# Reordered tokens and half-width keys in the first attention of a two-layer decoder kernel

## The chip, the cores and the metric

The kernel runs on one core of one Trainium2 chip. The time is the device time of one execution in microseconds (us), as the median of several runs. A profile is one execution taken by the hardware profiler.

## The reference

One sequence of 256 tokens, width 2048, two layers in float32. What matters here is the attention of the first layer, a mixture of three dilated windows with 8 heads of width 128 each:

```python
DILATED_GROUPS = ((128, 1), (512, 4), (2048, 16))     # window, distance
qkv = (xn @ w_in).reshape(B, S, 3, G * Hg, dh)        # G = 3 groups, Hg = 8 heads
q, k, v = rope(q) * dh ** -0.5, rope(k), v
for g, (window, dil) in enumerate(DILATED_GROUPS):
    idx = t[:, None] - dil * jnp.arange(window // dil + 1)[None, :]     # keys t, t - dil, ...
    s = where(idx >= 0, q[g] . k[g][idx], NEG_INF)
    lse = logsumexp(s); out = exp(s - lse) @ v[g][idx]
o = sum over g of softmax(lse over g) * out           # one softmax over all three groups' keys
h = h + o.reshape(S, Hg * dh) @ w_out
```

Then the first layer's MLP (2048 to 8192 and back) and gate, the shared keys and values, the second attention, its MLP and gate, and a last norm. With 256 tokens the second group sees the earlier keys whose distance is a multiple of 4, the third those at a multiple of 16, the first all keys up to 128 back.

## The kernel before

All large products are split: a float32 weight is cast to fp32r ("whi", ScalarE, line 198) and the rest is kept as "wlo" (VectorE, line 204), and activations are split likewise into two halves of one tile ("xa"). A weight comes in blocks of 128 x 1024 (512 KB), issued on SP's queue in program order (`load`, line 186). `Program.run` goes through a list of steps, keeps the loads some blocks ahead and the casts and splits three to four blocks ahead of the matmuls, and lets generators of other work advance by one `yield` between blocks. The schedule is written by hand: the instructions of each engine run in the order in which the program issues them. `prog.until` advances the generators until a condition holds.

x lies feature-major in SBUF, as eight tiles `xp[j]` of 128 features x (2 x 256 tokens). It is loaded once (`load_x`, line 180), squared and split at the start, and the out-projection later adds to it in place.

The first attention: `v_unit(0)` first, then for each head six `single` units (queries and keys of three groups, 16 blocks of 128 rows, lines 327 and 329), with the previous head's `a_scores` behind unit 1, `a_transpose` behind unit 3 and `a_pv` behind unit 4. Value units of 512 columns (`token_major`, lines 418 to 420) stand between heads: unit 1 after head 0, 2 after head 1, 3 after head 3, 4 after head 4, 5 in head 7. Value columns are ordered head by head, three groups each, so that a unit holds four (head, group) pairs. The rows of v for tokens 0 to 127 are kept split ("v0", two parts), those for 128 to 255 plain ("v1").

Tokens are in natural order. With two halves of 128 tokens, queries of the first half see only keys of the first, queries of the second see both. For each group the scores are a plain f32 product of 128 x 128 for the first half (line 717) and one of 128 x 256 for the second (line 718), 1152 columns of probabilities in all. They are masked (line 727), exponentiated (732), scaled (736), transposed on TensorE (746 to 749), copied out and split where both halves of the queries need them (754 to 757). `a_pv` makes, for each group, three split products with 256 columns (line 771: hi x hi, hi x lo, lo x hi) with the values of tokens 0 to 127 and one plain f32 product with 128 columns (769, 774) for queries and keys of the second half. `split_to` (448, 450) writes the head's output as hi and lo to "oT".

PSUM is two rings: "mm", four banks one at a time (`bank`), and "at", two pairs of banks (`banks2`). Scores and transposes take a pair and a bank each. The out-projection takes all four "mm" banks for its first 512 columns, and the last two heads' `a_pv` run behind its first and second weight block.

Of the kernel before, what the change touches and what calls it, by code (L numbers as in the profile page):

```python
# [10 lines left out]
F32 = mybir.dt.float32  # L11
F32R = mybir.dt.float32r
# [28 lines left out]

def f32(ap):
    return ap.bitcast(F32)


class Program:
# [87 lines left out]
def kernel(ctx: ExitStack, tc: tile.TileContext, a: dict, out: bass.AP):  # L134
# [40 lines left out]
    warm = const.tile([P, 1], F32, name="warm")  # L175
    nc.scalar.copy(warm, ones[:, :1])

    def load_x(j, half=None):
        c = slice(0, 2 * T) if half is None else slice(half * T, (half + 1) * T)
        nc.sync.dma_start(xp[j][:, c], a["xT"][:, j * 2 * T:(j + 1) * 2 * T][:, c])  # L180


    def load(n, src):
# [263 lines left out]
    def split_to(dst, src):  # L447
        nc.scalar.copy(dst[:, :T], src)
        yield
        nc.vector.tensor_sub(dst[:, T:], src, f32(dst[:, :T]))  # L450
# [194 lines left out]
    def start0():  # L645
        load_x(0, 0)
        load_x(0, 1)
        ps = bank()
        for _ in range(WARM_UP):
            nc.tensor.matmul(ps[:, :P], ones, ones, start=True, stop=True)  # L650
        open_pool("A")
        pa = cur["A"]
        cur["mA0"] = pa.tile([P, NGA * P], F32, name="mA0")
        cur["mA1"] = pa.tile([P, NGA * T], F32, name="mA1")

    def tables():
        nc.sync.dma_start(ident, a["ident"])
        nc.sync.dma_start(ropeC, a["ropeC"])
        nc.sync.dma_start(ropeS, a["ropeS"])
        nc.sync.dma_start(cur["mA0"], a["mA0"])  # L660
        nc.sync.dma_start(cur["mA1"], a["mA1"])
    prog.op(start0)

    def start_x(k):
# [4 lines left out]
    def square_pair(j):  # L669

        pa = cur["A"]
        if j == 0:
            cur["sum2"] = pa.tile([P, NGA * (P + T)], F32, name="p", tag="p")[:, :2 * T]
# [23 lines left out]
    def v_done(u, j, ps):  # L697
        while n_a0.r is None:
            yield
        v = cur["A"].tile([P, 512], F32, tag="v1", name="v1", bufs=3) if j else \  # L700
            cur["A"].tile([P, 2, 512], F32R, tag="v0", name="v0", bufs=3)
        col = n_a0.col[:, j:j + 1]
        nc.scalar.activation(v if j else v[:, 0], ps, AF.Identity, scale=col)
        if not j:
            yield
            nc.vector.scalar_tensor_tensor(v[:, 1], ps, col, f32(v[:, 0]), op0=ALU.mult, op1=ALU.subtract)
        va[u, j] = v

    sm = {}

    def a_scores(h):
        prog.until(lambda: ready.get(h) == 6)
        sb = banks2()
        flat, s0 = sb.rearrange("p a b -> p (a b)"), bank()
        for g in range(NGA):
            q, k = qk[h][:, g * T:(g + 1) * T], qk[h][:, (3 + g) * T:(4 + g) * T]
            nc.tensor.matmul(s0[:, g * P:(g + 1) * P], q[:, :P], k[:, :P], start=True, stop=True)
            nc.tensor.matmul(flat[:, g * T:(g + 1) * T], q[:, P:], k, start=True, stop=True)  # L718
        yield
        pa = cur["A"]  # L720
        p = pa.tile([P, NGA * (P + T)], F32, tag="p", name="p")
        s4 = pa.tile([P, 4], F32, tag="s4", name="s4", bufs=2)
        lo, parts = 0, []
        for j, (src, mask) in enumerate(((s0, cur["mA0"]), (flat, cur["mA1"]))):
            w = mask.shape[1]
            parts.append(p[:, lo:lo + w])
            nc.vector.tensor_tensor_reduce(out=parts[j], in0=src[:, :w], in1=mask, scale=-SCALE, scalar=3e38,
                                           op0=ALU.add, op1=ALU.min, accum_out=s4[:, j:j + 1])
            lo += w
        yield  # L730
        for j, d in enumerate(parts):
            nc.scalar.activation(d, d, AF.Exp, bias=s4[:, j:j + 1], scale=-1.0, accum_out=s4[:, 2 + j:3 + j])
        yield
        nc.vector.reciprocal(s4[:, 2:4], s4[:, 2:4])
        for j, d in enumerate(parts):
            nc.vector.tensor_scalar_mul(d, d, s4[:, 2 + j:3 + j])
        sm[h] = p

    def a_transpose(h):
        prog.until(lambda: h in sm)  # L740
        p = sm.pop(h)
        sb = banks2()
        flat, t0 = sb.rearrange("p a b -> p (a b)"), bank()
        w = NGA * P
        for g in range(NGA):
            nc.tensor.transpose(flat[:, g * T:g * T + P], p[:, g * P:(g + 1) * P], ident)
            nc.tensor.transpose(flat[:, g * T + P:(g + 1) * T], p[:, w + g * T:w + g * T + P], ident)
        for g in range(NGA):
            nc.tensor.transpose(t0[:, g * P:(g + 1) * P], p[:, w + g * T + P:w + (g + 1) * T], ident)
        yield  # L750
        pt = cur["A"].tile([P, NGA, 2, T], F32R, tag="pt", name="pt", bufs=2)
        pl = cur["A"].tile([P, w], F32, tag="pl", name="pl", bufs=2)
        early = flat[:, :NGA * T].rearrange("p (g t) -> p g t", g=NGA)
        nc.scalar.copy(pt[:, :, 0, :], early)
        nc.scalar.copy(pl, t0[:, :w])
        yield
        nc.vector.tensor_sub(pt[:, :, 1, :], early, f32(pt[:, :, 0, :]))
        sm[h, "T"] = pt, pl

    def a_pv(h, wide=False):  # L760
        units = {divmod(3 * h + g, 4)[0] for g in range(NGA)}
        prog.until(lambda: (h, "T") in sm and all((u, j) in va for u in units for j in range(2)))
        pt, pl = sm.pop((h, "T"))
        pv = (banks2()[:, 0, :] if wide else bank())[:, :T]
        for g in range(NGA):
            u, c = divmod(3 * h + g, 4)
            c = slice(c * P, (c + 1) * P)
            if g:
                nc.tensor.matmul(pv[:, P:], va[u, 1][:, c], pl[:, g * P:(g + 1) * P], start=False, stop=False)
            for vp, pp in ((0, 0), (0, 1), (1, 0)):  # L770
                nc.tensor.matmul(pv, va[u, 0][:, vp, c], pt[:, g, pp, :], start=g == vp == pp == 0,
                                 stop=g == NGA - 1 and vp == 1)
            if g == 0:
                nc.tensor.matmul(pv[:, P:], va[u, 1][:, c], pl[:, :P], start=False, stop=False)
# [12 lines left out]
    for h in range(HA):  # L787
        for i in range(6):
# [466 lines left out]
    return v.T.reshape(k // P, P, -1).transpose(1, 0, 2).reshape(P, -1)  # L1255


def _tables():
    f = np.float32
    inv = f(500000.0) ** (-np.arange(16, dtype=f) * f(2.0 / 32))  # L1260
# [6 lines left out]

    c, s = cs(t)
    tab = {"ropeC": c.T, "ropeS": s.T, "ident": np.eye(P, dtype=f)}
    cmp_pos = np.minimum(np.arange(16), 14) * 16 + 31  # L1270
# [5 lines left out]
    tab["mA0"] = np.concatenate([m[:P, :P] for m in add], 1)  # L1276
    tab["mA1"] = np.concatenate([m[P:, :] for m in add], 1)
# [9 lines left out]
def _layout(i):  # L1287
    a = dict(_tables())
    a["xT"] = _feature_major(i["x"][0])
    a["pT"] = np.stack([_feature_major(i["p"][l, 0]) for l in range(2)])  # L1290
# [5 lines left out]
    a["w_v"] = _quads(w[:, 2].transpose(0, 2, 1, 3).reshape(D, -1))  # L1296
# [37 lines left out]
```

## Time and profile before

| | |
|---|---|
| median of 3 runs | 2513.28 us (2513.19 to 2513.33) |
| profiled execution | 2514.11 us |
| its span | 2511.3 us |
| TensorE granted clock, mean | 0.999 |
| TensorE (PE) busy | 2500.4 us, 13497 matmul records |
| VectorE (DVE) busy | 1662.3 us |
| ScalarE (ACT) busy | 1351.0 us |
| DMA | 466.10 MB, mean 186 GB/s |

How to read the rows: PE is TensorE's matmuls, PEld its weight loads, which overlap the matmuls; SPq is the sequencer that issues transfers. "mm<-qk" means that tile mm is written from tile qk, L717 is line 717 of the kernel before. A plain f32 matmul appears as two records, an fp32r one and a transpose as one. Matmuls are pipelined, so a record's duration reaches into the next one. A timeline row has start, duration, engine, line, operation, tiles and shape, and "xN" merges N records. A row of the waits has the total in us, the number of times, and the longest. A row of a source line has the shortest, median and longest duration in ns, then the first and last start. A row of windows has the stretch, its length, the busy us (with the number of instructions) of PE, PEld, DVE, ACT and POOL, the granted clock, the DMA engines' share and GB/s.

### The profile page before, as it was taken

How to read it: one execution, taken by the hardware profiler on the slowest of the kernel's cores; microseconds unless marked ns; L12 is line 12 of the kernel's file. 1: busy time of each engine (PE TensorE's matmuls, PEld its weight loads, DVE VectorE, ACT ScalarE, POOL GpSimd, SP SyncE). 2: the span in 40 equal slices, each digit the busy share in tenths (PEclk: the TensorE clock that was granted, in tenths of full speed). 3: DMA queues.
4: the chain of work that ended last, by engine and by line, in shares of the span. 5: the costliest groups of instructions: out<-in, count | busy, mean ns of one | idle time of the engine just before them, and what ended most of it. 6: DMA issues, size and time to landing. Idle time of an engine off the chain costs nothing.

```text
span 2511.3 us, 36082 instructions
## 1 busy us (share of the span) xinstructions
PE 2500.4 (100%) x13497; PEld 2156.5 (86%) x13497; DVE 1662.3 (66%) x2808; ACT 1351.0 (54%) x2168; POOL 10.4 (0%) x24
## 2 busy tenths in 40 slices
PE   9999999999999999999999999999999999999998
PEld 8888888888888888888888889888888888888887
DVE  7766677865465565566787989766546556556676
ACT  6444444554454453455564788755545445445455
POOL 0000000000000000000000000000000000000000
PEclk9999999999999999999999999999999999999999
DMA  7555545556555655555565753455555655665553
GB/s 272 172 179 178 175 161 181 173 188 193 193 188 193 191 192 193 192 192 185 186 195 189 243 163 121 141 191 190 192 192 188 193 192 192 193 192 190 182 189 121
DMA packets 130111, 466.10 MB, mean 186 GB/s; under 512 B 14608, under 2 KB 15888, under 8 KB 129936
## 3 DMA queue, kind: packets, MB, share of 16 engines
q1 hardware_dynamic: 129264, 462.68, 56.6%
q8 instruction: 105, 1.72, 0.3%
q0 software_dynamic: 528, 1.07, 0.2%
q14 instruction: 70, 0.57, 0.1%
q10 hardware_dynamic: 144, 0.07, 0.0%
HBM read 461.65 MB, written 2.10 MB: 185 GB/s over the span
## 4 chain that ended last, share of the span: by engine, by line
PE 99%; DVE 0%; DMA 0%; SPq 0%; ACT 0%; issue 0%; DVEq 0%
PE mm L327 22%; PE at L327 17%; PE mm L329 11%; PE at L329 9%; PE mm L418 6%; PE mm L420 6%; PE mm L419 6%; PE at L420 5%; PE at L418 5%; PE at L419 5%; PE at L1180 0%; PE at L718 0%; PE mm L1204 0%; PE mm L938 0%; PE mm L939 0%; DMA raw<-in_w_v 0%
## 5 line engine op out<-in xcount | busy, mean ns | idle before, releaser
L204 DVE TENSOR_TENSOR wlo<-raw,whi 128x1024 fp32r<-128x1024 f32 (+1 forms) x875 | 1065.7, 1219 | 634.3 <-PE at L420 131.5
L198 ACT CAST whi<-raw 128x1024 fp32r<-128x1024 f32 (+1 forms) x875 | 919.8, 1052 | 880.4 <-PE at L327 198.9
L327 PE MATMUL mm<-xa,whi 128*128 128x512 f32 x2176 | 756.4, 396 | 0.0
L329 PE MATMUL mm<-xa,wlo 128*128 128x256 f32 x2176 | 587.9, 278 | 0.0
L327 PE MATMUL at<-xa,whi 128*128 128x512 f32 x1648 | 573.7, 393 | 0.0
L327 PEld LDWEIGHTS mm<-xa,whi 128*128 128x128 f32 x2176 | 401.4, 188 | 85.1 <-issue 0.4
L329 PE MATMUL at<-xa,wlo 128*128 128x256 f32 x1648 | 458.5, 278 | 0.0
L329 PEld LDWEIGHTS mm<-xa,wlo 128*128 128x128 f32 x2176 | 409.4, 188 | 9.7
L327 PEld LDWEIGHTS at<-xa,whi 128*128 128x128 f32 x1648 | 308.7, 187 | 70.0
L329 PEld LDWEIGHTS at<-xa,wlo 128*128 128x128 f32 x1648 | 310.2, 188 | 0.1
L418 PE MATMUL at<-whi,h 128*128 128x512 f32 x512 | 199.5, 390 | 0.0
L418 PE MATMUL mm<-whi,h 128*128 128x512 f32 x512 | 199.4, 389 | 0.0
L419 PE MATMUL mm<-whi,h 128*128 128x512 f32 x512 | 199.2, 389 | 0.0
L420 PE MATMUL mm<-wlo,h 128*128 128x512 f32 x512 | 199.2, 389 | 0.0
L420 PE MATMUL at<-wlo,h 128*128 128x512 f32 x512 | 199.2, 389 | 0.0
L419 PE MATMUL at<-whi,h 128*128 128x512 f32 x512 | 199.2, 389 | 0.0
L420 PEld LDWEIGHTS at<-wlo,h 128*128 128x128 f32 x512 | 96.1, 188 | 20.0
L420 PEld LDWEIGHTS mm<-wlo,h 128*128 128x128 f32 x512 | 96.1, 188 | 20.0
L418 PEld LDWEIGHTS mm<-whi,h 128*128 128x128 f32 x512 | 96.1, 188 | 19.9
L419 PEld LDWEIGHTS at<-whi,h 128*128 128x128 f32 x512 | 96.1, 188 | 19.8
L418 PEld LDWEIGHTS at<-whi,h 128*128 128x128 f32 x512 | 96.1, 188 | 19.8
L419 PEld LDWEIGHTS mm<-whi,h 128*128 128x128 f32 x512 | 96.1, 188 | 19.6
(315 smaller groups left out, 2529.5 us busy)
## 6 DMA issues: line engine op xcount, KB each, us to landing
raw<-in_w SPq DMA_DIRECT2D x512, 512.0 KB, 3.6
raw<-in_w_qk SPq DMA_DIRECT2D x96, 512.0 KB, 3.5
raw<-in_w_gate SPq DMA_DIRECT2D x56, 512.0 KB, 4.0
raw<-in_w_kv SPq DMA_DIRECT2D x48, 512.0 KB, 4.3
raw<-in_w_v SPq DMA_DIRECT2D x46, 512.0 KB, 3.6
raw<-in_w_q SPq DMA_DIRECT2D x32, 512.0 KB, 4.4
raw<-in_w_oB SPq DMA_DIRECT2D x32, 512.0 KB, 3.5
raw<-in_w_oA SPq DMA_DIRECT2D x16, 512.0 KB, 3.5
```

What stands on the lines that cost most here:

```text
L198: nc.scalar.copy(hi[:, c], t[:, c])
L204: nc.vector.tensor_sub(lo[:, c], t[:, c], f32(hi)[:, c])
L327: nc.tensor.matmul(ps, hi[:, col:col + P], rhs, start=first, stop=False)
L329: nc.tensor.matmul(ps[:, :T], lo[:, col:col + P], rhs[:, :T], start=False, stop=last)
L418: nc.tensor.matmul(st[j], xh, wh, start=k == 0, stop=False)
L419: nc.tensor.matmul(st[j], xl, wh, start=False, stop=False)
L420: nc.tensor.matmul(st[j], xh, wl, start=False, stop=k == KT - 1)
```

## The change

The first attention takes the tokens in another order: first those whose number leaves 0 or 1 when divided by 4, then those that leave 2 or 3. Keys at a distance that is a multiple of 4 then lie in the query's own half, so the second and third group's scores become 128 x 128 for each half; the first group's become 128 x 256 for each half. A head has 1024 columns of probabilities, 512 for each half of the queries, side by side in two banks. The values of the first group are needed by both halves of queries and are kept split for both halves of tokens; those of the two other groups are kept plain. The value columns are reordered to that end: units 0 and 3 hold the first group of four heads, units 1, 2, 4 and 5 the other two groups of two heads.

x is loaded in the new order (xTA), with its rotary tables (ropeCA, ropeSA) and one mask table mA, and is loaded again in natural order between the units of heads 2 and 3, as are the rotary tables behind the out-projection. The output of a head is put back into natural order when it is copied out of PSUM. The squares at the start use the tiles of oT in place of those of v1.

```diff
+def halved(ap):
+    return ap.rearrange("p (h a s) -> p a h s", h=2, s=2)
+
+def plain(ap):
+    return ap.rearrange("p (a h s) -> p a h s", h=2, s=2)
...
-        nc.sync.dma_start(xp[j][:, c], a["xT"][:, j * 2 * T:(j + 1) * 2 * T][:, c])
+        nc.sync.dma_start(xp[j][:, c], a[order][:, j * 2 * T:(j + 1) * 2 * T][:, c])
...
-        cur["mA0"] = pa.tile([P, NGA * P], F32, name="mA0")
-        cur["mA1"] = pa.tile([P, NGA * T], F32, name="mA1")
+        cur["mA"] = pa.tile([P, 2, 2 * T], F32, name="mA")
...
-        s = pa.tile([P, 2 * T], F32, tag="v1", name="v1", bufs=3) if j else total
+        s = f32(pa.tile([P, 2 * T], F32R, tag="oT", name="oT", bufs=HA)) if j else total
...
-        v = cur["A"].tile([P, 512], F32, tag="v1", name="v1", bufs=3) if j else \
-            cur["A"].tile([P, 2, 512], F32R, tag="v0", name="v0", bufs=3)
-        nc.scalar.activation(v if j else v[:, 0], ps, AF.Identity, scale=col)
-        if not j:
+        if j == 0:
+            va[u] = cur["A"].tile([P, 2, 512], F32, tag="v12", name="v12", bufs=2) if u % 3 else \
+                cur["A"].tile([P, 2, 2, 512], F32R, tag="v0", name="v0", bufs=2)
+        nc.scalar.activation(v[:, j] if u % 3 else v[:, j, 0], ps, AF.Identity, scale=col)
+        if not u % 3:
             yield
...
     def a_scores(h):
-        flat, s0 = sb.rearrange("p a b -> p (a b)"), bank()
-        for g in range(NGA):
-            nc.tensor.matmul(s0[:, g * P:(g + 1) * P], q[:, :P], k[:, :P], start=True, stop=True)
-            nc.tensor.matmul(flat[:, g * T:(g + 1) * T], q[:, P:], k, start=True, stop=True)
+        for j in range(2):
+            own = slice(j * P, (j + 1) * P)
+            for g in (1, 2, 0):
+                nc.tensor.matmul(sb[:, j, T + (g - 1) * P:T + g * P] if g else sb[:, j, :T], q[:, own],
+                                 k[:, own] if g else k, start=True, stop=True)
...
     def a_transpose(h):
-        flat, t0 = sb.rearrange("p a b -> p (a b)"), bank()
-        for g in range(NGA):
-            nc.tensor.transpose(flat[:, g * T:g * T + P], p[:, g * P:(g + 1) * P], ident)
-            nc.tensor.transpose(flat[:, g * T + P:(g + 1) * T], p[:, w + g * T:w + g * T + P], ident)
-        for g in range(NGA):
-            nc.tensor.transpose(t0[:, g * P:(g + 1) * P], p[:, w + g * T + P:w + (g + 1) * T], ident)
+        tr = banks2()
+        for i in range(4):
+            for j in range(2):
+                nc.tensor.transpose(tr[:, i // 2, (i % 2 * 2 + j) * P:(i % 2 * 2 + j + 1) * P],
+                                    p[:, j, i * P:(i + 1) * P], ident)
...
     def a_pv(h, wide=False):
-            if g:
-                nc.tensor.matmul(pv[:, P:], va[u, 1][:, c], pl[:, g * P:(g + 1) * P], start=False, stop=False)
+        def far(j):
             for vp, pp in ((0, 0), (0, 1), (1, 0)):
-                nc.tensor.matmul(pv, va[u, 0][:, vp, c], pt[:, g, pp, :], start=g == vp == pp == 0,
+                nc.tensor.matmul(pv, va[u0][:, j, vp, c], pt[:, j, pp, :], start=j == vp == pp == 0,
-            if g == 0:
-                nc.tensor.matmul(pv[:, P:], va[u, 1][:, c], pl[:, :P], start=False, stop=False)
+        far(0)
+        for g in range(2):
+            n = slice((h % 2 * 2 + g) * P, (h % 2 * 2 + g + 1) * P)
+            for j in range(2):
+                nc.tensor.matmul(pv[:, j * P:(j + 1) * P], va[u1][:, j, n], pl[:, g * T + j * P:g * T + (j + 1) * P],
+                                 start=False, stop=False)
+        far(1)
...
-        yield from split_to(o, pv)
+        nc.scalar.copy(plain(o[:, :T]), halved(pv))
+        yield
+        nc.vector.tensor_sub(plain(o[:, T:]), halved(pv), plain(f32(o[:, :T])))
...
+            if h in (2, 3) and i < 4:
+                prog.op(lambda j=4 * h - 8 + i: load_x(j, order="xT"))
...
+    def plain_rope():
+        nc.sync.dma_start(ropeC, a["ropeC"])
+        nc.sync.dma_start(ropeS, a["ropeS"])
+    prog.op(plain_rope)
```

More of the change, by code (lines that the diff above doesn't have):

```diff
@@ L176, with load_x @@
     nc.scalar.copy(warm, ones[:, :1])
-    def load_x(j, half=None):
+    def load_x(j, half=None, order="xTA"):
         c = slice(0, 2 * T) if half is None else slice(half * T, (half + 1) * T)
-        nc.sync.dma_start(xp[j][:, c], a["xT"][:, j * 2 * T:(j + 1) * 2 * T][:, c])
+        nc.sync.dma_start(xp[j][:, c], a[order][:, j * 2 * T:(j + 1) * 2 * T][:, c])
     def load(n, src):
@@ L652, in start0 @@
         pa = cur["A"]
-        cur["mA0"] = pa.tile([P, NGA * P], F32, name="mA0")
-        cur["mA1"] = pa.tile([P, NGA * T], F32, name="mA1")
+        cur["mA"] = pa.tile([P, 2, 2 * T], F32, name="mA")
     def tables():
         nc.sync.dma_start(ident, a["ident"])
[L658 to L661, printed above, removed]
+        nc.sync.dma_start(ropeC, a["ropeCA"])
+        nc.sync.dma_start(ropeS, a["ropeSA"])
+        nc.sync.dma_start(cur["mA"].rearrange("p j t -> p (j t)"), a["mA"])
     prog.op(start0)
@@ L672, in square_pair @@
         if j == 0:
-            cur["sum2"] = pa.tile([P, NGA * (P + T)], F32, name="p", tag="p")[:, :2 * T]
+            cur["sum2"] = pa.tile([P, 2, 2 * T], F32, name="p", tag="p")[:, 0]
         total = cur["sum2"]
-        s = pa.tile([P, 2 * T], F32, tag="v1", name="v1", bufs=3) if j else total
+        s = f32(pa.tile([P, 2 * T], F32R, tag="oT", name="oT", bufs=HA)) if j else total
         nc.scalar.activation(s, xp[j], AF.Square)
@@ L699, in v_done @@
             yield
-        v = cur["A"].tile([P, 512], F32, tag="v1", name="v1", bufs=3) if j else \
-            cur["A"].tile([P, 2, 512], F32R, tag="v0", name="v0", bufs=3)
-        col = n_a0.col[:, j:j + 1]
-        nc.scalar.activation(v if j else v[:, 0], ps, AF.Identity, scale=col)
-        if not j:
+        if j == 0:
+            va[u] = cur["A"].tile([P, 2, 512], F32, tag="v12", name="v12", bufs=2) if u % 3 else \
+                cur["A"].tile([P, 2, 2, 512], F32R, tag="v0", name="v0", bufs=2)
+            ready["v", u] = 0
+        v, col = va[u], n_a0.col[:, j:j + 1]
+        nc.scalar.activation(v[:, j] if u % 3 else v[:, j, 0], ps, AF.Identity, scale=col)
+        if not u % 3:
             yield
-            nc.vector.scalar_tensor_tensor(v[:, 1], ps, col, f32(v[:, 0]), op0=ALU.mult, op1=ALU.subtract)
-        va[u, j] = v
+            nc.vector.scalar_tensor_tensor(v[:, j, 1], ps, col, f32(v[:, j, 0]), op0=ALU.mult, op1=ALU.subtract)
+        ready["v", u] += 1
     sm = {}
@@ L713, in a_scores @@
         sb = banks2()
-        flat, s0 = sb.rearrange("p a b -> p (a b)"), bank()
-        for g in range(NGA):
-            q, k = qk[h][:, g * T:(g + 1) * T], qk[h][:, (3 + g) * T:(4 + g) * T]
-            nc.tensor.matmul(s0[:, g * P:(g + 1) * P], q[:, :P], k[:, :P], start=True, stop=True)
-            nc.tensor.matmul(flat[:, g * T:(g + 1) * T], q[:, P:], k, start=True, stop=True)
+        for j in range(2):
+            own = slice(j * P, (j + 1) * P)
+            for g in (1, 2, 0):
+                q, k = qk[h][:, g * T:(g + 1) * T], qk[h][:, (3 + g) * T:(4 + g) * T]
+                nc.tensor.matmul(sb[:, j, T + (g - 1) * P:T + g * P] if g else sb[:, j, :T], q[:, own],
+                                 k[:, own] if g else k, start=True, stop=True)
         yield
         pa = cur["A"]
-        p = pa.tile([P, NGA * (P + T)], F32, tag="p", name="p")
+        p = pa.tile([P, 2, 2 * T], F32, tag="p", name="p")
         s4 = pa.tile([P, 4], F32, tag="s4", name="s4", bufs=2)
[L723 to L727, printed above, removed]
+        for j in range(2):
+            nc.vector.tensor_tensor_reduce(out=p[:, j], in0=sb[:, j], in1=cur["mA"][:, j], scale=-SCALE, scalar=3e38,
                                            op0=ALU.add, op1=ALU.min, accum_out=s4[:, j:j + 1])
-            lo += w
         yield
-        for j, d in enumerate(parts):
-            nc.scalar.activation(d, d, AF.Exp, bias=s4[:, j:j + 1], scale=-1.0, accum_out=s4[:, 2 + j:3 + j])
+        for j in range(2):
+            nc.scalar.activation(p[:, j], p[:, j], AF.Exp, bias=s4[:, j:j + 1], scale=-1.0,
+                                 accum_out=s4[:, 2 + j:3 + j])
         yield
         nc.vector.reciprocal(s4[:, 2:4], s4[:, 2:4])
-        for j, d in enumerate(parts):
-            nc.vector.tensor_scalar_mul(d, d, s4[:, 2 + j:3 + j])
+        for j in range(2):
+            nc.vector.tensor_scalar_mul(p[:, j], p[:, j], s4[:, 2 + j:3 + j])
         sm[h] = p
@@ L741, in a_transpose @@
         p = sm.pop(h)
-        sb = banks2()
-        flat, t0 = sb.rearrange("p a b -> p (a b)"), bank()
-        w = NGA * P
-        for g in range(NGA):
-            nc.tensor.transpose(flat[:, g * T:g * T + P], p[:, g * P:(g + 1) * P], ident)
-            nc.tensor.transpose(flat[:, g * T + P:(g + 1) * T], p[:, w + g * T:w + g * T + P], ident)
-        for g in range(NGA):
-            nc.tensor.transpose(t0[:, g * P:(g + 1) * P], p[:, w + g * T + P:w + (g + 1) * T], ident)
+        tr = banks2()
+        for i in range(4):
+            for j in range(2):
+                nc.tensor.transpose(tr[:, i // 2, (i % 2 * 2 + j) * P:(i % 2 * 2 + j + 1) * P],
+                                    p[:, j, i * P:(i + 1) * P], ident)
         yield
-        pt = cur["A"].tile([P, NGA, 2, T], F32R, tag="pt", name="pt", bufs=2)
-        pl = cur["A"].tile([P, w], F32, tag="pl", name="pl", bufs=2)
-        early = flat[:, :NGA * T].rearrange("p (g t) -> p g t", g=NGA)
+        pt = cur["A"].tile([P, 2, 2, T], F32R, tag="pt", name="pt", bufs=2)
+        pl = cur["A"].tile([P, 2 * T], F32, tag="pl", name="pl", bufs=2)
+        early = tr[:, 0].rearrange("p (b t) -> p b t", b=2)
         nc.scalar.copy(pt[:, :, 0, :], early)
-        nc.scalar.copy(pl, t0[:, :w])
+        nc.scalar.copy(pl, tr[:, 1])
         yield
@@ L760, in a_pv @@
     def a_pv(h, wide=False):
-        units = {divmod(3 * h + g, 4)[0] for g in range(NGA)}
-        prog.until(lambda: (h, "T") in sm and all((u, j) in va for u in units for j in range(2)))
+        u0, u1 = h // 4 * 3, h // 4 * 3 + 1 + h % 4 // 2
+        prog.until(lambda: (h, "T") in sm and ready.get(("v", u0)) == ready.get(("v", u1)) == 2)
         pt, pl = sm.pop((h, "T"))
         pv = (banks2()[:, 0, :] if wide else bank())[:, :T]
-        for g in range(NGA):
-            u, c = divmod(3 * h + g, 4)
-            c = slice(c * P, (c + 1) * P)
-            if g:
-                nc.tensor.matmul(pv[:, P:], va[u, 1][:, c], pl[:, g * P:(g + 1) * P], start=False, stop=False)
-            for vp, pp in ((0, 0), (0, 1), (1, 0)):
-                nc.tensor.matmul(pv, va[u, 0][:, vp, c], pt[:, g, pp, :], start=g == vp == pp == 0,
-                                 stop=g == NGA - 1 and vp == 1)
-            if g == 0:
-                nc.tensor.matmul(pv[:, P:], va[u, 1][:, c], pl[:, :P], start=False, stop=False)
+        c = slice(h % 4 * P, (h % 4 + 1) * P)
+        def far(j):
+            for vp, pp in ((0, 0), (0, 1), (1, 0)):
+                nc.tensor.matmul(pv, va[u0][:, j, vp, c], pt[:, j, pp, :], start=j == vp == pp == 0,
+                                 stop=j == vp == 1)
+        far(0)
+        for g in range(2):
+            n = slice((h % 2 * 2 + g) * P, (h % 2 * 2 + g + 1) * P)
+            for j in range(2):
+                nc.tensor.matmul(pv[:, j * P:(j + 1) * P], va[u1][:, j, n], pl[:, g * T + j * P:g * T + (j + 1) * P],
+                                 start=False, stop=False)
+        far(1)
         yield
         o = cur["A"].tile([P, 2 * T], F32R, tag="oT", name="oT", bufs=HA)
-        yield from split_to(o, pv)
+        nc.scalar.copy(plain(o[:, :T]), halved(pv))
+        yield
+        nc.vector.tensor_sub(plain(o[:, T:]), halved(pv), plain(f32(o[:, :T])))
         oT[h] = o
@@ L1255, in _feature_major, with _order @@
     return v.T.reshape(k // P, P, -1).transpose(1, 0, 2).reshape(P, -1)
+def _order():
+    return np.arange(T).reshape(T // 4, 2, 2).transpose(1, 0, 2).ravel()
 def _tables():
@@ L1269, in _tables @@
     tab = {"ropeC": c.T, "ropeS": s.T, "ident": np.eye(P, dtype=f)}
+    order = _order()
+    tab["ropeCA"], tab["ropeSA"] = c.T[:, order], s.T[:, order]
     cmp_pos = np.minimum(np.arange(16), 14) * 16 + 31
@@ L1275, in _tables @@
     add = [np.where(v, 0.0, NEG).astype(f) for v in valid]
-    tab["mA0"] = np.concatenate([m[:P, :P] for m in add], 1)
-    tab["mA1"] = np.concatenate([m[P:, :] for m in add], 1)
+    far, *near = (m[np.ix_(order, order)] for m in add)
+    halves = [slice(j * P, (j + 1) * P) for j in range(2)]
+    tab["mA"] = np.concatenate([np.concatenate([far[r]] + [m[r, r] for m in near], 1) for r in halves], 1)
     causal = np.where(d >= 0, 0.0, NEG).astype(f)
@@ L1289, in _layout @@
     a["xT"] = _feature_major(i["x"][0])
+    a["xTA"] = _feature_major(i["x"][0][_order()])
     a["pT"] = np.stack([_feature_major(i["p"][l, 0]) for l in range(2)])
@@ L1295, in _layout @@
     a["w_qk"] = _singles(w[:, :2].transpose(0, 3, 1, 2, 4).reshape(D, -1))
-    a["w_v"] = _quads(w[:, 2].transpose(0, 2, 1, 3).reshape(D, -1))
+    v = w[:, 2]
+    a["w_v"] = _quads(np.concatenate([t.reshape(D, -1) for h in (0, 4) for t in
+                                      (v[:, 0, h:h + 4], v[:, 1:, h:h + 4].transpose(0, 2, 1, 3))], 1))
     a["w_oA"] = _quads(i["a_w_out"][0])
```

## Prediction

> **What bounds the kernel now.** First the head of the profile's page: busy shares and the chain that ended last.
>
> ```profile
> span 2511.3 us, 36082 instructions
> PE 2500.4 (100%) x13497; PEld 2156.5 (86%) x13497; DVE 1662.3 (66%) x2808; ACT 1351.0 (54%) x2168; POOL 10.4 (0%) x24
> PE 99%; DVE 0%; DMA 0%; SPq 0%; ACT 0%; issue 0%; DVEq 0%
> ```
>
> TensorE (PE) is busy for the whole span and carries 99% of the chain. A busy PE could still be waiting inside, so next the list of PE's waits; this is all of it:
>
> ```profile
> PE mm L650 <- DVE ones L170: 1.1, 1, 1.1
> PE at L420 <- DVE wlo L204: 0.4, 1, 0.4
> PE at L1131 <- DVE ko L450: 0.3, 1, 0.3
> PE at L1132 <- DVE pt L1190: 0.2, 1, 0.2
> ```
>
> In 2511 us PE waits 2.0 us, and none of it is in the first attention: L650 and L420 are the start, the other two the second attention. So the time is the sum of PE's slots, and the price of a matmul is the distance from its start to the start of the next one. The durations in the rows overlap and are no price. VectorE, ScalarE and DMA matter only if the change makes PE wait. The sum is made on the profiled execution (2514.11 us, of which the span is 2511.3) and carried over to the median, 2513.28.
>
> **The PE work of one head.** PE's timeline, head 0, scores (L717, L718), then the first matmul that follows:
>
> ```profile
> 93.79 0.38 PE L717 MATMUL mm<-qk 128*128 128x128 f32 x2
> 94.01 0.60 PE L718 MATMUL at<-qk 128*128 128x256 f32 x2
> 94.45 0.38 PE L717 MATMUL mm<-qk 128*128 128x128 f32 x2
> 94.67 0.60 PE L718 MATMUL at<-qk 128*128 128x256 f32 x2
> 95.10 0.38 PE L717 MATMUL mm<-qk 128*128 128x128 f32 x2
> 95.32 0.60 PE L718 MATMUL at<-qk 128*128 128x256 f32 x2
> 95.57 0.58 PE L327 MATMUL mm<-xa,whi 128*128 128x512 f32 x1
> ```
>
> Each f32 product is two passes ("x2"). A product with 128 columns takes 94.01 - 93.79 = 0.22 us, one with 256 takes 94.45 - 94.01 = 0.44. Before, a head has three of each: 1.98 us. After, two halves each have two products with 128 columns (distances 4 and 16, own half only) and one with 256: four of 0.22 and two of 0.44, 1.76 us. The block still ends with a 256, so the hand-over to L327 stays. Saved: 0.22.
>
> The transposes of the probabilities:
>
> ```profile
> 107.07 0.27 PE L746 MATMUL at<-ident,p 128*128 128x128 f32 x1
> 107.18 0.27 PE L747 MATMUL at<-ident,p 128*128 128x128 f32 x1
> ...
> 107.72 0.49 PE L749 MATMUL mm<-ident,p 128*128 128x128 f32 x3
> 107.97 0.47 PE L327 MATMUL mm<-xa,whi 128*128 128x512 f32 x1
> ```
>
> One takes 107.18 - 107.07 = 0.11 us. There are nine of them; after, eight, since the probabilities are 1024 columns wide and not 1152. Saved: 0.11.
>
> The product with the values:
>
> ```profile
> 116.38 0.52 PE L771 MATMUL mm<-pt,v 128*128 128x256 f32 x3
> 116.73 0.38 PE L774 MATMUL mm<-pl,v 128*128 128x128 f32 x2
> 116.95 0.39 PE L769 MATMUL mm<-pl,v 128*128 128x128 f32 x2
> 117.09 0.60 PE L771 MATMUL mm<-pt,v 128*128 128x256 f32 x3
> 117.53 0.38 PE L769 MATMUL mm<-pl,v 128*128 128x128 f32 x2
> 117.67 0.60 PE L771 MATMUL mm<-pt,v 128*128 128x256 f32 x3
> 118.11 0.40 PE L327 MATMUL mm<-xa,whi 128*128 128x512 f32 x1
> ```
>
> Three split products with 256 columns (L771) take 0.35 us as the first group (116.38 to 116.73) and 0.44 behind an f32 product (117.09 to 117.53); a plain f32 product with 128 columns takes 0.22 (116.73 to 116.95), or 0.14 as the last one before L771, which then starts early and pays it back in its 0.44. Before: 118.11 - 116.38 = 1.73. After, the order is three split products, four plain ones, three split ones: 0.35 + 3 x 0.22 + 0.14 + 0.44 = 1.59. Saved: 0.14. One group of three and one change between the two kinds go, one plain product comes.
>
> **Sum.** 0.22 + 0.11 + 0.14 = 0.47 us a head, 8 heads: 3.76 us. The built program has the 24 fewer matmul instructions that this implies (8 transposes, 16 products with the values), and behind the attention PE's order is the same to the end. Nothing late is next on PE: no stall goes, only slots, and what is late next is the matmul behind them. Profiled 2514.11 - 3.76 = 2510.35; median 2513.28 - 3.76 = 2509.5 us. That is 0.15%, inside the 0.2% that I take as what a measurement of this kernel can tell from no change. If the three rounded terms are each 0.03 off the same way, the saving lies between 3.0 and 4.5.
>
> **What lies beside PE, at nothing.** Scores, exponentials, scaling and evacuations go from 1152 to 1024 columns on VectorE and ScalarE, the split part of the transposed probabilities from 768 to 512, and the value units need four low parts and not six. All of that shrinks. Four things grow.
>
> *The second load of x.* Eight transfers of 256 KB, in natural order, issued on SP between the weight loads of heads 2 and 3; behind each one on SP's queue waits the next weight block, and for it ScalarE, VectorE, then PE. They overwrite x, whose last readers (squares and splits) ran in head 0, so they wait for nothing.
>
> ```profile
> 0.00:60.00 60.00, 58.54 (x302) 49.75 (x303) 42.15 (x63) 40.28 (x59) 0.20 (x4) 1.00 0.80 276
> 160.00:260.00 100.00, 100.00 (x564) 87.12 (x563) 68.71 (x129) 44.70 (x62) 0.00 (x0) 1.00 0.51 171
> raw<-in_w_qk SPq DMA_DIRECT2D x96, 512.0 KB, 3.5
> x<-in_xT SPq DMA_DIRECT2D x7, 256.0 KB, 6.6
> ```
>
> The first two rows are stretches of time, whose last figures are clock, DMA share and GB/s; the others are the loads, with KB and us to landing. In the stretch of heads 2 and 3 (second row) the DMA engines are 51% busy at 171 GB/s. 2.1 MB more in about 100 us makes 192 GB/s, below the 276 of the first row, which holds the same load of x. One transfer at that 276 GB/s holds the queue for 0.95 us. The cover is the lead of the weight buffers before PE; with no lead at all it would cost 8 x 0.95 = 7.6 us. The far end: if a weight block behind a transfer lands as late as x did in the crowded start (6.6 for 3.5), 3.1 us, 8 x 3.1 = 24.8 less the lead each time. I take 0, since this stretch is like the half-idle second row and not like the first.
>
> *The low part of the first value unit for both halves.* It falls into VectorE's queue behind the rotations of head 0, and three weight splits stand behind it:
>
> ```profile
> 75.61 0.73 DVE L706 SCALAR_TENSOR_TENSOR v<-at,col,v 128x512 fp32r<-128x512 f32 x1
> 76.27 3.47 DVE L204 TENSOR_TENSOR wlo<-raw,whi 128x1024 fp32r<-128x1024 f32 x3
> 80.48 0.39 PE L420 MATMUL mm<-wlo,xa 128*128 128x512 f32 x1
> ```
>
> One more of 0.73 moves the three by that much. The first of them ends at about 76.27 + 3.47/3 = 77.43, and PE takes it at 80.48 (counted in weight blocks): 3 us of lead, 2.3 are left. Cost 0; without the lead 0.7 once. I take this, behind a burst, for the tightest place of the weights after the start.
>
> *The output of a head is written back in token order*, read out of PSUM in pairs, 128 columns apart. No strided read of PSUM is in the trace; the nearest rows are the plain evacuation and a strided copy in SBUF:
>
> ```profile
> L919 ACT CAST z<-zf x32: 402/427/454, 1381.1 to 1434.5; 128x120 fp32r<-128x120 f32 x32
> 450.60 0.37 ACT L448 CAST oT<-at 128x256 fp32r<-128x256 f32 x1 [3.21 <-PE at L771]
> 451.01 0.42 DVE L450 TENSOR_TENSOR oT<-at,oT 128x256 fp32r<-128x256 f32 x1 [0.85 <-ACT oT L448]
> 453.19 0.40 PE L327 MATMUL mm<-oT,whi 128*128 128x512 f32 x1
> ```
>
> Contiguous, 256 columns take 0.37; strided, 120 take 0.43, so at worst 256 take 0.43 x 256/120 = 0.92, 2.5 times as long. Only the last head is pressed: its output is done at 451.01 + 0.42 = 451.43, and the fourth weight block of the out-projection, which reads it first, begins at 453.19, 1.76 us later. At 2.5 times, both operations add 0.55 + 0.63 = 1.18: still hidden. Pairs are still runs, so I take a value near the plain row, and 0 for PE.
>
> The Trainium skill, "SBUF — State Buffer" (section "Door 1: The DMA port swizzle", on "cachelines"), says that PSUM has lines of 8 bytes and that non-contiguous access there slows matmuls significantly. Here ScalarE and VectorE read, and each pair is just one such line. No row here shows that effect, and the rule gives no factor; by it the sum would be that of the rival "evacuation" below.
>
> *The natural rotary tables* are two small loads issued after the out-projection; their only readers are the factors of the second layer, behind the whole MLP and gate: 0.
>
> **The rivals.**
> *Long runs of plain products (slower).* Before, at most two 128-column f32 products follow each other (L774, L769: four passes); after, four do in each head's value block: eight passes. A weight load of such a product:
>
> ```profile
> 444.38 0.30 PEld L774 LDWEIGHTS at<-pl,v 128*128 128x128 f32 x2
> 444.60 0.30 PEld L769 LDWEIGHTS at<-pl,v 128*128 128x128 f32 x2
> ```
>
> Two loads fill 0.30 us though they come 0.11 apart, so one lasts 0.19, longer than its pass (0.11). If loads get ahead only over short runs, the eight passes take 0.19 each: 8 x 0.08 x 8 heads = 5.1 us, 2514.6, slower than before by 1.3. It decides from the fifth pass of a run on. Against it: the loads hold their 0.11 over four passes without slowing.
> *Reload of x (slower).* With no lead +7.6, 2517.1; at the far end, with the 2.3 us of lead left each time, 8 x 0.8 = 6.4, 2515.9, and with neither 24.8, 2534.3. It decides once a transfer delays a weight block by more than its lead. For it: SP is one queue in order. Against it: the DMA share above, 0.95 against 2.3, and a list of PE's waits without a DMA in it.
> *Evacuation.* From 1.76/0.79 = 2.2 times longer in addition (3.2 times in all) the out-projection waits; at four times 2.37 - 1.76 = 0.6, once: 2510.1.
> *More goes than the slots.* The heads no longer take a bank each for scores and transposes, and the tables at the start are 64 KB less. PE waits only 2.0 us in all, so even all of it would give 2507.5.
>
> **How the numbers follow.** The slots alone: 0.82. Long runs 0.03, reload 0.06 (half of it above 2518.3), evacuation 0.03, more than the slots 0.06. Predicted 2509.5. The range is 2508.5 to 2512.0: below it reaches to the upper end of the saving and half of the last rival's gain, above it takes the lower end (2510.3), the evacuation and a reload that costs a quarter of its price. Faster by over 0.2% (below 2508.25) is the last rival, 0.06; slower by over 0.2% (above 2518.3) is the upper half of the reload, 0.03; within 0.2% the rest, 0.91.
>
> **What would show it.** In the profile after: PE still 100% and no new row among its waits between 90 and 460 us; a score block of 1.76 us up to its hand-over, eight transposes of 0.11, a value block of 1.59; its plain products 0.22 apart; everything behind 460 us earlier by 3 to 4.5 us and unchanged in itself. Wrong is the forecast if plain products stand 0.38 apart, if PE waits for a weight cast in heads 2 and 3, or if the out-projection waits for the last head.

## The result and the profile after

The changed kernel takes 2510.31 us (median of 22 runs, 2509.67 to 2511.1); the kernel before, on the same chip in turn, 2513.53 (22 runs, 2512.84 to 2514.28). The ratio is 0.9987, 95% interval 0.9981 to 0.9993: 3.2 us less, forecast were 3.76. The profiled execution took 2509.67 us. The head of the page after:

```profile
span 2507.9 us, 36064 instructions
PE 2496.9 (100%) x13481; PEld 2153.1 (86%) x13481; DVE 1657.0 (66%) x2806; ACT 1348.4 (54%) x2168; POOL 10.4 (0%) x24
```

PE is busy throughout as before, with 16 records less. The list of PE's waits after, complete (lines are now 11 to 18 higher):

```profile
PE mm L661 <- DVE ones L181: 1.1, 1, 1.1
PE at L429 <- ACT whi L209: 0.4, 1, 0.4
PE at L1149 <- DVE ko L461: 0.3, 1, 0.3
PE at L431 <- DVE wlo L215: 0.3, 1, 0.3
PE at L1150 <- DVE pt L1208: 0.2, 1, 0.2
```

2.3 us in place of 2.0; the second and fourth rows are the first weight blocks, and nothing in heads or out-projection waits. PE's timeline of head 0: scores (L730), transposes (L755), values (L775 split, L781 plain), each with the matmul behind it:

```profile
93.33 1.92 PE L730 MATMUL at<-qk 128*128 128x128 f32 x12
94.89 0.58 PE L338 MATMUL mm<-xa,whi 128*128 128x512 f32 x1
...
106.38 1.03 PE L755 MATMUL at<-ident,p 128*128 128x128 f32 x8
107.17 0.48 PE L338 MATMUL mm<-xa,whi 128*128 128x512 f32 x1
...
115.58 0.52 PE L775 MATMUL mm<-pt,v 128*128 128x256 f32 x3
115.93 1.05 PE L781 MATMUL mm<-pl,v 128*128 128x128 f32 x8
116.74 0.60 PE L775 MATMUL mm<-pt,v 128*128 128x256 f32 x3
117.18 0.40 PE L338 MATMUL mm<-xa,whi 128*128 128x512 f32 x1
```

From start to start the blocks take 1.56, 0.79 and 1.60 us; before they took 1.78 (95.57 - 93.79), 0.90 and 1.73. Over the eight heads the traces give 1.66, 0.87 and 1.05 us less: 3.58 us. The eight passes of L781 fill 0.81 us, 0.11 each (the last one shorter, as before): long runs of plain products don't slow down.

**Where the rest went.** Between the blocks PE does the same products in the same order, and yet these stretches, up to the last matmul, are 0.72 us longer. The same weight block of head 1, twelve products, first before and then after:

```profile
120.90 0.39 PE L327 MATMUL mm<-xa,whi 128*128 128x512 f32 x1
121.13 0.27 PE L329 MATMUL mm<-xa,wlo 128*128 128x256 f32 x1
...
122.98 0.39 PE L327 MATMUL mm<-xa,whi 128*128 128x512 f32 x1
```

```profile
119.65 0.40 PE L338 MATMUL mm<-xa,whi 128*128 128x512 f32 x1
119.88 0.28 PE L340 MATMUL mm<-xa,wlo 128*128 128x256 f32 x1
...
121.77 0.40 PE L338 MATMUL mm<-xa,whi 128*128 128x512 f32 x1
```

Six pairs of a hi and a lo product lie between first and last row: 2.08 us before, 2.12 after. In nearly all weight blocks of both traces a pair takes either 346.7 or 353.3 ns on average. Of the 505 blocks in this order 24 before and 29 after lie between, most of them in the second out-projection. In the heads, one of the two holds over several weight blocks and changes only where other work comes between (scores, transposes, values, a value unit). A block of eight pairs at the slow spacing costs 0.053 us more. I counted the slow blocks of each trace, those whose second to seventh pair average 350 ns or more; "first out-projection" includes the eight blocks right behind it:

| kernel | slow blocks: heads, first out-projection, whole kernel | from the second weight block of head 0 to the last matmul, us |
|---|---|---|
| before | 29, 17, 89 | 2470.08 |
| after | 40, 23, 108 | 2467.21 |

19 more slow blocks would be 1.0 us; the stretches lost 0.72 as measured. Matched product by product, the weight blocks take 0.85 us more, since several of those that change do so by less than 0.053, and all other products 0.13 less. So the change takes 3.58 us out and gives 0.72 back: 2.87 in the trace from the second weight block on. What lies ahead of that (the first loads and splits) varied by 1.1 us between the traces of this study that share its instructions, 31.8 to 32.9 us, so no effect of the change can be read from it. The medians differ by 3.22 us; the other 0.35 is not explained.

### The profile page after: what moved, and what is told of

Its sections match the earlier page's. It is cut to its first block, busy times and chain, and to the rows that moved or that the text cites. A ratio compares the mean times of both kernels' runs of the same rounds, so it can differ in the third digit from the quotient of the medians.

```text
span 2507.9 us, 36064 instructions
## 1 busy us (share of the span) xinstructions
PE 2496.9 (100%) x13481; PEld 2153.1 (86%) x13481; DVE 1657.0 (66%) x2806; ACT 1348.4 (54%) x2168; POOL 10.4 (0%) x24
## 4 chain that ended last, share of the span: by engine, by line
PE 99%; DVE 0%; DMA 0%; SPq 0%; ACT 0%; issue 0%; DVEq 0%
PE mm L338 22%; PE at L338 17%; PE mm L340 11%; PE at L340 9%; PE mm L429 6%; PE mm L430 6%; PE mm L431 6%; PE at L431 5%; PE at L429 5%; PE at L430 5%; PE at L730 1%; PE at L1198 0%; PE mm L1222 0%; PE mm L956 0%; PE mm L957 0%; PE at L755 0%
```

## The experiments

The run without the reload, the one with three reloads, the doubled scores and the first one with another order ran beside the kernel before at 2513.28 us (33 runs); the kernel after is taken at 2510.3.

**Without the reload of x.** One edit:

```diff
-            if h in (2, 3) and i < 4:
-                prog.op(lambda j=4 * h - 8 + i: load_x(j, order="xT"))
```

> Leaves out the second load of x (the eight transfers in natural order between the units of heads 2 and 3), so the rest of the network adds to x in the wrong token order. Slots theory (the reload is hidden): the changed kernel's time, 2510.3 us, within 0.5. Rival (the reload eats part of the saving): faster than the changed kernel, by up to 8 x 0.95 = 7.6 us; the 0.5 us that the measured saving lacks against 3.76 would come back, above all in heads 2 and 3.

2510.19 us (11 runs), ratio 0.9988 (0.9979 to 0.9996). The stretch in the table: 2467.18, as after (2467.21). The windows of the stretch of the reload, after and without it:

```profile
150.00:250.00 100.00, 100.00 (x564) 87.06 (x563) 68.78 (x128) 45.04 (x62) 0.00 (x0) 1.00 0.57 192
```

```profile
150.00:250.00 100.00, 100.00 (x564) 87.06 (x563) 68.11 (x126) 45.04 (x62) 0.00 (x0) 1.00 0.53 174
```

The reload shows in the DMA columns (57% and 192 GB/s for 53% and 174); PE does the same 564 matmuls. The two VectorE instructions fewer are the window's edge, since this trace begins 0.7 us later. The reload is hidden, and the lost part of the saving isn't there.

**The reload in one piece, once and three times.** All transfers are issued behind the first unit of head 2. The edit shown is that of the single reload; the triple one, which was run first, loops over `3 * list(range(KT // 2))`:

```diff
-            if h in (2, 3) and i < 4:
-                prog.op(lambda j=4 * h - 8 + i: load_x(j, order="xT"))
+            if h == 2 and i == 0:
+                for j in range(KT // 2):
+                    prog.op(lambda j=j: load_x(j, order="xT"))
```

> The second load of x once, but all eight transfers at one place behind the first unit of head 2: 7.6 us of the queue at 276 GB/s in one piece. Theory of a finite cover (14 us or more by the run with 24): no wait of TensorE there, 2510.3 within 0.7. Rival (a cover of one or two transfers): 2512 to 2517.

Measured 2510.08 us (10 runs; the kernel before beside it 2513.19), and no PE wait there. The eight in one piece are covered.

> The same reload, but all at one place (behind the first unit of head 2) and three times over: 24 transfers of 256 KB, 24 x 0.95 = 22.8 us of the queue at 276 GB/s. Slots theory with a cover of finite lead: a weight block there is issued some 17 to 20 us before TensorE uses it and needs 3.5 us to land, so the cover is about 14 to 17 us and TensorE waits 5 to 9 us once, 2515 to 2519 us. Theory that a reload never matters: 2510.3. Theory that there is no cover: 22.8 more less the 7.6 that the spread reload would already cost, 2525.

Measured 2516.86 us (11 runs), ratio 1.0015 (1.0006 to 1.0024): 6.6 us more than after, inside the 5 to 9. The waits of all engines between 140 and 185 us:

```profile
ACT whi L209 <- DMA raw<-in_w_qk: 15.4, 3, 14.0
DVE et L346 <- ACT es L344: 14.7, 3, 11.1
PEld at L755 <- DVE p L746: 5.0, 2, 4.8
PE at L755 <- DVE p L746: 4.5, 1, 4.5
```

The rows are a chain. ScalarE waits 14.0 us for a weight block, behind it in its queue wait the copies of finished sums (L344), VectorE waits 11.1 us for one of those, and behind that in its own queue stands the scaling of the probabilities (L746), for which PE's transposes wait 4.5. PE ran dry not through its weights but through the softmax, which shares two queues with them.

That the time fell inside the 5 to 9 is luck, for both terms behind it were too large. SP issued the 24 transfers in 15.8 us (144.07 to 159.91), 0.66 each and not 0.95, so the queue was held 15.8 us and not 22.8; with 4.5 of wait the cover was about 11 us (an estimate) and not 14 to 17. By the same 0.66 the eight in one piece are 5.3 us and not 7.6.

```profile
144.07 15.44 SPq L191 DMA_DIRECT2D x<-in_xT  x24
159.91 14.28 SPq L197 DMA_DIRECT2D raw<-in_w_qk  x6
```

The wait is not all of the loss either: the stretch of the table is 2473.35, 6.1 us more than after. The eight transposes behind the wait and the clock in that window:

```profile
170.92 2.15 PE L755 MATMUL at<-ident,p 128*128 128x128 f32 x8 [4.48 <-DVE p L746]
172.72 0.78 PE L338 MATMUL mm<-xa,whi 128*128 128x512 f32 x1
171.00:174.00 3.00, 3.00 (x12) 2.59 (x13) 2.97 (x8) 1.68 (x3) 0.00 (x0) 0.50 0.55 178
```

They take 1.80 us (170.92 to 172.72) for 0.79 after, and the next few products are slower too: the granted clock was 0.50 here, and 0.99 from 174 to 178 us. This stall of PE cost about a third more than its own length.

**The near scores twice.** The products at distances 4 and 16 are written a second time into the same place:

```diff
-            for g in (1, 2, 0):
+            for g in (1, 2, 1, 2, 0):
```

> The scores at distances 4 and 16 are computed twice into the same place: four more plain products with 128 columns for each head. Slots theory: 4 x 0.22 x 8 = 7.0 us more than the changed kernel, 2517.3 us, and runs of eight passes still at 0.11 each. Theory that long runs of plain products fall to 0.19 a pass: the score block's runs of eight passes each take 1.52 in place of 0.88, 7.0 + 2 x 8 x 0.08 x 8 = 17.2 more. Theory that PE's slots are partly hidden: less than 7.0.

2517.47 us (11 runs): 7.2 more than after. PE's timeline of head 0:

```profile
94.25 2.81 PE L730 MATMUL at<-qk 128*128 128x128 f32 x20
96.71 0.58 PE L338 MATMUL mm<-xa,whi 128*128 128x512 f32 x1
```

2.46 us for 1.56: four more products, 0.9 us, 0.22 each. The price of a slot is paid in full, and runs of eight passes keep it.

**Another order right behind a block.** `mm_tiles` can take two hi and then two lo products (`run=2`); the kernel before does that, among other places, in the first weight block of heads 0, 1, 2, 4 and 5. Here it does so behind each attention block too:

```diff
...
-                mm_tiles(hi, lo, tiles, run if c == 0 or both else 1)
+                mm_tiles(hi, lo, tiles, run if c == 0 or both else after_mid)
...
-                   ... run=2 if i == 0 and h in UNIT_AHEAD else 1, mid=
+                   ... run=2 if i == 0 and h in UNIT_AHEAD or i == 5 and 0 < h < HA - 1 else 1,
+                   after_mid=2 if h and i in (1, 3) else 1, mid=
```

> Behind each attention block of heads 0 to 6 the next weight block takes two hi products and then two lo products in turn (as the first block of heads 0, 1, 2, 4 and 5 already does) in place of hi, lo, hi, lo. In the trace of the changed kernel a pair of hi and lo takes either 346.7 or 353.3 ns, and which of the two it is changes at the attention blocks and holds until the next. Theory that the order of two and two sets the faster spacing: some 44 weight blocks of 8 pairs at 6.7 ns, up to 2.3 us less, 2508.0 us. Rival (the spacing is set by something else): within 0.7 of 2510.3, with the slow stretches at other places.

2508.3 us (11 runs), ratio 0.998 (0.9971 to 0.9989): 2.0 us less than after. All 40 slow blocks of the heads are gone (68 left in the kernel), and the stretch of the table is 2465.32, 1.89 less. So the spacing costs about what was counted (40 x 0.053 = 2.1). Whether the order sets the fast spacing as such was for the next two.

**The same edit in the kernel before.**

> The kernel before with only the edit of the previous run (two hi and two lo products in turn right behind each attention block of heads 0 to 6). Theory that the changed kernel saves its slots in full (1.66 + 0.87 + 1.05 = 3.58 us by the traces) and gives about 0.9 back by more weight blocks at the slow spacing (40 in the heads against 29, and 22 against 17 behind them): all of the heads' 29 slow blocks go, 29 x 0.053 = 1.5 us, 2511.7 us, and the distance to the changed kernel with the same edit (2508.3) is 3.4 to 3.9. Rival (what the saving lacks lies elsewhere, in waits or in the start): 2513.3 within 0.5, or a distance below 3.0.

2514.15 us (11 runs) beside 2513.19 (26 runs), ratio 1.0004 (0.9995 to 1.0012): not faster. The trace has 37 slow blocks in the heads in place of 29, 99 in all, and the stretch is 2470.66, 0.58 longer. The theory that two and two in turn sets the fast spacing is wrong: behind the kernel-before's blocks of scores and transposes it leads into the slow one. My expected distance of 3.4 to 3.9 to the changed kernel with the same edit was missed as well (5.85). But the sum behind it holds: by the traces the distance is 2470.66 - 2465.32 = 5.34 us, and 3.58 of slots and 31 slow blocks (99 less 68) of 0.053 make 5.2.

**The same edit in both out-projections too.** In addition to the edit of the heads:

```diff
...
-                                  for f in range(4) for i in range(2)], 1 if c else run)
+                                  for f in range(4) for i in range(2)], 2 if c in twos else 1 if c else run)
...
-                 single_ring and q == 0, True, 2 if q == 1 else 1)
+                 single_ring and q == 0, True, 2 if q == 1 else 1,
+                 [0] + [c + 1 for c in hooks] if q == 0 else ())
```

> The changed kernel with the same edit, and in both out-projections too, for the first weight block and for each block that stands right behind an attention block. Theory that two and two in turn right behind a foreign block sets the fast spacing until the next one: the 22 slow blocks of the first out-projection and the 28 of the second go, 50 x 0.053 = 2.7 us, 2505.6 us. Rival (it sets the spacing in the units of the heads only, since the second quad of the out-projection already begins so and stays slow): 2508.3 within 0.5.

2507.19 us (10 runs), ratio 0.9976 (0.9966 to 0.9985). The first out-projection has lost its 23 slow blocks, 1.1 us by the stretch; the second, with the blocks right behind it, keeps its 30. Half right again: the edit turned one place and not the other.

**Repeats, and two and two everywhere.** The changed kernel, the previous one and a third beside the kernel before at 2513.37 (25 runs). The edit of the third, in `mm_tiles` of the previous kernel, is one line, `run = 2`.

> The changed kernel once more, beside the next two on the same chip. All theories: 2510.3 within 0.5; from the second weight block of head 0 to the last matmul 2467.2 us, as in the four traces of it and of its variants that leave TensorE's work alone (2467.18 to 2467.21), while the start differs by up to 1 us.

2510.17 us (11 runs), ratio 0.9987 (0.9978 to 0.9996); the stretch 2467.15, a hair outside the four traces before.

> The changed kernel with two hi and two lo products in turn behind foreign blocks, once more: 2507.2 within 0.5, and 3.0 us less than the changed kernel on the same chip.

2507.25 us (9 runs), ratio 0.9975 (0.9966 to 0.9985), 2.9 us less than the changed kernel on the same chip. This kernel is the fastest of the study.

> Two hi and two lo products in turn in every weight block of this kind in the whole kernel. Theory that the spacing of hi, lo, hi, lo has two states of its own (2.773 and 2.826 us for a weight block) and two and two has only one (2.777): the 45 slow blocks still left in the previous kernel go, 45 x 0.05 = 2.2 us, and some 430 fast blocks pay 0.003 each, 1.3 us: 2506.3. Rival (two and two is no state of its own and only shifts what follows): a slower spacing in long stretches, above 2508.

2511.62 us (11 runs), ratio 0.9993 (0.9984 to 1.0002): a miss, on the rival's side. In the MLP a weight block in this order takes 2.787 us where hi, lo, hi, lo takes 2.773. The 431 blocks that had the 346.7 ns spacing and changed their order take 5.6 us more in all, the 45 that had been counted as slow take 1.2 less, and the stretch grew from 2464.26 (the second run of the previous kernel) to 2468.64, 4.4. The 2.777 that I had taken was from single blocks; a long run is slower.

**The evacuation in single columns.** The output of a head is read out of PSUM in single columns 128 apart, not in pairs, which leaves the tokens in another order than the reference's:

```diff
-        nc.scalar.copy(plain(o[:, :T]), halved(pv))
+        by_one = lambda ap: ap.rearrange("p (h a) -> p a h", h=2)
+        in_row = lambda ap: ap.rearrange("p (a h) -> p a h", h=2)
+        nc.scalar.copy(in_row(o[:, :T]), by_one(pv))
...
-        nc.vector.tensor_sub(plain(o[:, T:]), halved(pv), plain(f32(o[:, :T])))
+        nc.vector.tensor_sub(in_row(o[:, T:]), by_one(pv), in_row(f32(o[:, :T])))
```

> The changed kernel with the output of a head read out of PSUM in single columns, 128 columns apart, in place of pairs, which gives another token order than the reference's. Theory that a strided read of PSUM by ScalarE and VectorE costs nothing: 0.37 and 0.42 us as in the changed kernel, and no wait in the out-projection. Theory of lines of 8 bytes (two columns): each line is fetched twice, up to twice as long, 0.7 and 0.8 us; even then the out-projection should not wait, since 0.8 more is less than the 1.76 us of slack.

A single run: 2510.82 us, stretch 2467.20. The evacuation on ScalarE by its source line (shortest, median, longest in ns), in pairs (after) and in single columns:

```profile
L786 ACT CAST oT<-mm x6: 373/373/374, 117.4 to 372.0; 128x256 fp32r<-128x256 f32 x6
L786 ACT CAST oT<-at x2: 373/373/373, 442.6 to 447.0; 128x256 fp32r<-128x256 f32 x2
```

```profile
L788 ACT CAST oT<-mm x6: 373/373/374, 118.5 to 373.1; 128x256 fp32r<-128x256 f32 x6
L788 ACT CAST oT<-at x2: 373/373/373, 443.7 to 448.1; 128x256 fp32r<-128x256 f32 x2
```

373 ns in each, and 0.37 before, when it was contiguous. VectorE's subtraction takes 416 to 424 ns in both. A strided read of PSUM cost the two engines nothing here. The Trainium skill ("SBUF — State Buffer", section "Door 1: The DMA port swizzle") says that PSUM has lines of 8 bytes and that non-contiguous access there slows matmuls significantly. These two engines' reads were not slowed; no run here tries matmuls.

## Why the prediction was right

Forecast were 2509.5 us, measured 2510.31, inside the range and the way that was forecast. By its steps:

- *PE's slots are the time.* Right: without the reload, with the reload in one piece, or with another evacuation the stretch is the same to 0.03 us, and four added products a head cost their full slots (7.1 us by the stretch).
- *The three terms.* 0.22, 0.11 and 0.14 a head were forecast; 0.21, 0.11 and 0.13 were measured, 3.58 for 3.76. The score block "of 1.76 us" was counted with the whole last product; the next matmul starts inside it, before as after, so from start to start it is 1.56. Both sides of the difference had the same error, so the 0.22 is not touched by it.
- *"Behind the attention PE's order is the same to the end", hence unchanged in itself.* This step failed, in size and not in direction. The order is the same, but its spacing isn't fixed by the order: 19 more weight blocks run at the slow spacing, and 0.72 us of the saving go back, 0.42 between the blocks of the heads and 0.30 behind. So the traces save 2.87, just less than the 3.0 that was forecast as the least; the time stayed in the range all the same, which had room for a partly paid reload and a slower evacuation. The timeline of the kernel before would have shown it: the same pair (L327, L329) took 346.7 ns in some weight blocks of the trace before and 353.3 in others.
- *The reload at nothing.* Right; 192 GB/s was worked out and measured. The limit was misplaced: I had the weights' lead as the cover, and what ran dry first, with 24 transfers, was the softmax in the queues of ScalarE and VectorE. The price of a transfer, 0.95 us, came from the stretch at 276 GB/s; back to back they took 0.66.
- *The evacuation at nothing, and the low part of the value unit in the burst.* Right: 0.37 as before, and no wait of PE in either place.
- *Long runs of plain products.* The rival is refuted: 0.11 a pass over eight passes, in the values and in the doubled scores.
- *More goes than the slots.* Not seen: PE's waits are 2.3 us for 2.0, all at the start and in the second attention, as before.

Open: what sets the spacing. It isn't the order of two and two as such: the same edit turned the changed kernel's heads to fast and led the kernel before's into slow. It isn't the length of the foreign work alone either. In the trace before, the scores were followed by the slow spacing among the units of heads 1, 2, 4 and 5 and by the fast one among those of 3 and 6, though they are the same products and fast blocks stood ahead of them in all six. In the trace after, each of the 20 score, transpose and value blocks in the heads was followed by the other spacing than stood ahead of it. It isn't the reload's transfers, since the stretch stays the same without them.

## What to carry to other kernels

Where one engine is busy from end to end with no waits, price a change in its start-to-start slots, each kind from its own row, and the sum comes out to a few per cent; the durations of the pipelined matmuls (273 ns for a pass of 110) would have given more than twice the price. Before calling everything else on that engine unchanged, compare the same instruction's spacing at several places of the one trace: if it has two values, a change elsewhere can move stretches from one to the other. And ask of a burst of transfers which in-order queue the late block stands in, and what else stands behind it.

## What was not expected of the hardware

Identical sequences of a 512-column and a 256-column fp32r matmul ran at 346.7 or 353.3 ns a pair, at a granted clock of 1.00, and held the slow one over as many as 16 weight blocks in a row. Turning the blocks at the long spacing in the heads and in the first out-projection was worth 2.9 us (2510.17 to 2507.25), nearly as much as the change itself. A ScalarE copy of 256 columns out of PSUM took 373 ns whether contiguous, in pairs or in single columns 128 apart. Behind a wait of 4.5 us PE ran at a granted clock of 0.50 for about 3 us, and eight transposes took 1.80 us in place of 0.79.
